# A Hymba layer in fp32 on one core: memory projections first, norms in place with later transposes, GLA decays one pair ahead

## The chip, the core and the metric

The kernel runs on one core of one Trainium2 chip. The metric is the device time of one execution in microseconds (us); given are the median of three executions and one execution under the hardware profiler. The engines are TensorE (PE in the profile, PEld its weight loads), VectorE (DVE), ScalarE (ACT), GpSimd (POOL) and SyncE (SP, which here only issues DMAs).

## The reference

One decoder layer over 512 tokens of width 2048, everything in float32:

```python
xn = rms_norm(h, attn_norm_g)
proj = xn @ w_in
(gq, gk, gv, gg, ga, fq, fk, fv, fg, ff, mq, mg) = jnp.split(proj, _split_points(), axis=-1)
log_a = jax.nn.log_sigmoid((ga @ gla_a_w2 + gla_a_b)) / GLA_TAU
gla_o = gla_chunked(gq, gk, gv, log_a)               # 8 heads, keys of 64, values of 128
fq_h, fk_h = rms_norm(fq, fox_q_norm_g), rms_norm(fk, fox_k_norm_g)
log_f = jax.nn.log_sigmoid(ff + fox_f_b)
fox_o = forgetting_attention(fq_h, fk_h, fv, log_f)   # 4 heads, causal softmax with decays
mn = rms_norm(mem, mem_norm_g)                        # 256 memory tokens
mk, mv = jnp.split(mn @ w_mem_kv, 2, axis=-1)
mk, mq_h = rms_norm(mk, mem_k_norm_g), rms_norm(mq, mem_q_norm_g)
mem_o = softmax(mq_h @ mk.T / sqrt(128)) @ mv         # 4 heads, no mask
o = rms_norm(concat([gla_o, fox_o, mem_o]), out_norm_g)  # per head of 128
gate = concat([silu(gg), sigmoid(fg), sigmoid(mg)])
h = h + (o * gate) @ w_out
u = relu(rms_norm(h, mlp_norm_g) @ w_up)
h = h + (u * u) @ w_down
```

## The kernel before

**Arithmetic.** A float32 product is made of three matmuls of a rounded format (`mm3`, lines 156 to 158): high by high, high by low, low by high. Every weight tile is loaded raw by SP (line 147), rounded by ACT into its high part (148), and DVE takes the remainder as the low part (149). A projection step multiplies one 128-row slice of x by one weight tile: 12 matmuls of 128x512.

**Stages.** First `project` makes gk and gq, and meanwhile `x_sums(0)` and `x_sums(1)` load x again and add its quarters, which the next stage needs. Then four `in_pair` products (gla values, and fq with fk) run by a seven-product scheme whose sums and differences DVE makes. A narrow projection `small` follows. From there to the output projection two generators are interleaved by the code: `projections()` yields after each 12 matmuls, and `steps()` runs the attention work, each `yield n` asking for n such pieces before its next step. After that come the output projection (out0 and on) and the two MLP products.

**What sets the order.** PE runs its matmuls in the order in which the code wrote them, frozen by dependencies. DVE, ACT, POOL and SP run in the order that the tile framework's scheduler gave by priorities: a weight's load and split are put forward (`AHEAD`). An engine does not look past the instruction at its head. In this middle stage there are two buffers of split weights (`n_hl = 2`) and three of raw ones. PSUM is in two pools of four banks: `gbank` for projections, `abank` for attention.

**The projections** are fv, mq, mkv (memory keys and values, 16 tiles of 12 matmuls), then the four gates gg0, gg1, fg and mg. After each gate group `gate` (line 1014) scales it out of PSUM into z, applies log-sigmoid (574, 575), an exponential and for gg a product with z (1018), multiplies the head outputs (1019), and forms the quarter sums s (243) that the output projection needs; some go out to DRAM. Its z uses the buffers of bT and eb.

**The attention steps.** `first_steps` scales gk and gq (651) and makes lf, the log of FoX's forget gates (656). `gla` runs over four chunks of 128 tokens. `decays` makes cumulative logs b; then seven block sizes ("levels") are handled in pairs: `level` takes differences (719, 720), an exponential on ACT (721) and products with q and k (ql 725, e 731); `level_scores` makes scores on PE (lp, 737) and `place_scores` copies them under a mask (746). Then o, the state st and, for chunks before the last, the next decays. `norms` and `turned_heads` normalize heads: four squares with sums on ACT, a reciprocal root on DVE and ACT (118 to 124), a product (590), and after some yields the transposes on PE (tps 603, ot 944) and a scaled copy by ACT (946). `Fox` and `Mem` are softmax attention in banks of logits: lg on PE, ls on DVE (841), p on ACT (890), its transposes pT (898), the product av (909). Memory's keys are normalized by `memory_norms`, which starts from squares of memory (199, 200) that each memory tile adds beside its projection. `place` fetches head sums back for the output projection.

Of the kernel before, what the change touches and what calls it, by code (L numbers as in the profile page):

```python
# [12 lines left out]
ALU = mybir.AluOpType  # L13
# [33 lines left out]
def hybrid_layer(  # L47
# [289 lines left out]
    def multiply(w, after, inside=None):  # L337
# [230 lines left out]

    def log_sigmoid(dst, z, e):
# [5 lines left out]
        V.scalar_tensor_tensor(dst, z, 0.0, e, op0=ALU.min, op1=ALU.subtract)  # L575
# [16 lines left out]
    def norms(srcs, gain, dsts, name, wait):  # L592

        for a in range(0, len(srcs), 2):
            r = head_rms(srcs[a : a + 2], f"{name}{a}")
            nrm = [tmp(f"nrm_{name}{a + i}", "tc") for i in range(2)]
            for i in range(2):
                normed(nrm[i], srcs[a + i], r[:, 4 * i : 4 * i + 4])
            yield wait
            for i in range(2):  # L600
                tps = abank(f"tps_{name}{a + i}")
                for h in range(4):
                    T.transpose(tps[:, h * 128 : h * 128 + 128], nrm[i][:, h * 128 : h * 128 + 128], ident)
                A.activation(dsts[a + i], tps.rearrange("p (h t) -> p h t", h=4), AF.Copy, scale=gain)
# [35 lines left out]
    def first_steps():  # L640
        G.memset(gaT, 1.0)
        V.tensor_mul(gaT[:16, :], nps[32:48, :], rbx[32:48, :])
        lfT = tmp("lfT", "td")[:FH, :]
# [8 lines left out]
        yield 2  # L652
# [6 lines left out]
        g = decay_logs(0)  # L659
        yield from norms([o[:, t, 1024:1536] for t in range(NT)], gains[:, 0:1], tokens(fqT), "fq", 2)  # L660
# [9 lines left out]
        return g  # L670
# [40 lines left out]
    def level(c, li, bT):  # L711
# [5 lines left out]
        e = tmp(f"e_{c}_{B}", "ta")  # L717
# [3 lines left out]
        A.activation(e, e, AF.Exp)  # L721
        ql = qls[li % 2]
# [7 lines left out]

        V.tensor_mul(ev[:, :, :hb], ev[:, :, :hb], blocks_of(kTs[:, c, :], B)[:, :, :hb])
# [21 lines left out]
    def gla(g):  # L753
        state = tmp("state", "rbx")
        bT, eb, kd = decays(0, g)
        for c in range(NT):
# [3 lines left out]
            ready = [level(c, li, bT) for li in (0, 1)]  # L760
            yield 2 if c else 3
            for a in (0, 2, 4, 6):
# [3 lines left out]
                if a == 6:  # L766
# [15 lines left out]
                yield 3 if a in (0, 4) else 2  # L782
# [33 lines left out]
            if c == 0:  # L816
                yield from norms([o[:, t, 1536:2048] for t in range(NT)], g_fk, tokens(fkT), "fk", 1)
# [36 lines left out]
    class Mem:  # L854
# [12 lines left out]
        def v(self, s, h):  # L867
            return late["mv"][:, s, h * 128 : h * 128 + 128]
# [64 lines left out]
    def turned_heads(n, wait):  # L933

        ot = o[:, :, n * 512 : n * 512 + 512]
        for a in (0, 2):
            r = head_rms([ot[:, a + i, :] for i in range(2)], f"on_{n}_{a}")
            for i in range(2):
                normed(ot[:, a + i, :], ot[:, a + i, :], r[:, 4 * i : 4 * i + 4])
        yield wait  # L940
# [8 lines left out]
    mem_ready = []  # L949
    late = {}  # L950

    def memory_norms():
        mkv = bigt(1, [128, 2, 1024], "mkv")
        mkT = late["mkT"] = mkv[:, 0, :].rearrange("p (h m) -> p h m", h=MH)
        mv = late["mv"] = mkv[:, 1, :].rearrange("p (m c) -> p m c", m=MT)
        mqT = late["mqT"] = bigt(0, [128, 4, S], "mqT")
        mrstd = token_rstd(macc, MT, "mem")
        mks = room.rearrange("p (m c) -> p m c", m=MT)
        for m in range(MT):
            V.tensor_scalar(mks[:, m, :], mks[:, m, :], mrstd[:, m : m + 1], None, op0=ALU.mult)  # L960
            A.activation(mv[:, m, :], mraw[:, m, :], AF.Copy, scale=mrstd[:, m : m + 1])
        dsts = [mkT[:, :, m * 128 : m * 128 + 128] for m in range(MT)]
        yield from norms([mks[:, m, :] for m in range(MT)], g_mk, dsts, "mk", 2)
        yield 1
        yield from norms([o[:, t, 1536:2048] for t in range(NT)], gains[:, 1:2], tokens(mqT), "mq", 2)

    def steps():
        g = yield from first_steps()
        yield 2
        yield from gla(g)  # L970
        assert mem_ready
        yield 1
# [464 lines left out]
```

## Time and profile before

| quantity | value |
|---|---|
| median of 3 executions | 2209.38 us (2209.36 to 2211.11) |
| profiled execution | 2212.2 us |
| its span in the trace | 2210.5 us |
| PE, DVE, ACT, POOL busy | 2130.1, 1617.7, 1142.7, 195.5 us |
| mean clock granted to PE | 0.983 of full |

The span is from the first to the last instruction of the profiled execution. "Busy" leaves out waiting. A releaser, written with an arrow (`<-`), is the instruction on another engine that ended a wait.

### The profile page before, as it was taken

What the parts mean: (1) busy time and instruction counts of PE and PEld (TensorE: products, weight loads), DVE (VectorE), ACT (ScalarE), POOL (GpSimd) and SP (SyncE); (2) the same over time, 40 slices, a digit from 0 to 9 for tenths busy, and PEclk for the clock granted to TensorE, in tenths of its full rate; (3) what the DMA queues carried; (4) which work ended last, traced back from release to release, by engine and by line L of the source; (5) the groups of instructions that cost most, each with busy time, mean ns of one, the idle gap of its engine ahead of it and who ended that gap; (6) DMA issues with size and microseconds to landing.
All of it is one profiled execution on the core that took longest, in us unless ns stands there. A gap on an engine that the chain in (4) does not pass through costs nothing.

```text
span 2210.5 us, 25633 instructions
## 1 busy us (share of the span) xinstructions
PE 2130.1 (96%) x9746; PEld 1747.9 (79%) x9746; DVE 1617.7 (73%) x1711; ACT 1142.7 (52%) x1715; POOL 195.5 (9%) x239
## 2 busy tenths in 40 slices
PE   8999999897979989999999999999999999999999
PEld 7887688786767778878888888888788788788787
DVE  7689766865364498887677767769868768777875
ACT  6553442535365465655555555556645546546543
POOL 0433100000000003100000000000010000000000
PEclk9999999998989999999999999999999999999999
DMA  7443222421232566624534533445586677678654
GB/s 268 143 157 101 95 65 70 142 78 60 67 100 77 180 223 225 238 87 142 190 125 142 190 127 141 171 161 190 201 228 187 199 204 229 165 198 243 187 170 131
DMA packets 77988, 348.15 MB, mean 157 GB/s; under 512 B 9241, under 2 KB 11289, under 8 KB 56362
## 3 DMA queue, kind: packets, MB, share of 16 engines
q1 hardware_dynamic: 57770, 275.22, 36.0%
q0 software_dynamic: 20096, 71.31, 12.3%
q8 instruction: 76, 1.25, 0.2%
q14 instruction: 46, 0.38, 0.1%
HBM read 271.00 MB, written 75.50 MB: 157 GB/s over the span
## 4 chain that ended last, share of the span: by engine, by line
PE 79%; DVE 10%; DMA 4%; ACT 3%; issue 3%; SPq 0%; DVEq 0%; ACTq 0%
PE acc_up L156 9%; PE acc_up L158 9%; PE acc_up L157 9%; PE acc_dn L157 7%; PE acc_dn L158 7%; PE acc_dn L156 7%; PE acc_out L157 2%; PE acc_out L156 2%; PE acc_out L158 2%; DMA left1l<-op 2%; DVE hl_hl_in L333 2%; DVE hl_dn L333 1%; PE gg L156 1%; DVE raw_dn L295 1%; PE gg L158 1%
## 5 line engine op out<-in xcount | busy, mean ns | idle before, releaser
L333 DVE TENSOR_TENSOR hl_up<-raw_up,hl_up 128x1024 fp32r<-128x1024 f32 x224 | 271.8, 1223 | 144.0 <-ACT hl_up L333 143.8
L333 ACT CAST hl_up<-raw_up 128x1024 fp32r<-128x1024 f32 x224 | 235.3, 1052 | 256.2 <-PE acc_up L158 196.3
L333 DVE TENSOR_TENSOR hl_dn<-raw_dn,hl_dn 128x1024 fp32r<-128x1024 f32 x224 | 270.6, 1222 | 99.2 <-ACT hl_dn L333 98.4
L333 ACT CAST hl_dn<-raw_dn 128x1024 fp32r<-128x1024 f32 x224 | 234.6, 1054 | 209.3 <-PE acc_dn L158 160.2
L295 DVE TENSOR_TENSOR raw_dn<-raw_dn,raw_dn 128x2048 f32<-128x2048 f32 x64 | 146.1, 2287 | 15.9 <-DMA raw_dn<-in_w_down_dram 15.6
L295 DVE TENSOR_TENSOR raw_up<-raw_up,raw_up 128x2048 f32<-128x2048 f32 x64 | 145.2, 2269 | 0.2 <-DMA raw_up<-in_w_up_dram 0.2
L333 ACT CAST hl_out<-raw_out 128x1024 fp32r<-128x1024 f32 x56 | 58.6, 1052 | 56.9 <-PE acc_out L158 36.4
L1352 POOL DMA_DIRECT2D hd<-m x48 | 41.5, 865 | 518.4 <-ACT m L1351 518.4
L333 DVE TENSOR_TENSOR hl_out<-raw_out,hl_out 128x1024 fp32r<-128x1024 f32 x56 | 70.3, 1272 | 15.3 <-ACT hl_out L333 15.2
L1351 ACT COPY m<-acc_dn 128x512 f32<-128x512 f32 x96 | 54.5, 587 | 30.4 <-PE acc_dn L158 30.4
L1244 POOL DMA_DIRECT2D op<-u x32 | 17.1, 533 | 491.8 <-ACT u L1253 482.5
L156 PE MATMUL gg<-ahi_x,hl_gg 128*128 128x512 f32 x128 | 53.6, 418 | 6.6 <-DVE z_gg L1014 6.6
L157 PE MATMUL acc_dn<-hl_dn,left 128*128 128x512 f32 x128 | 50.3, 393 | 4.5 <-DVE hl_dn L333 4.5
L157 PE MATMUL acc_dn<-hl_dn,left0h 128*128 128x512 f32 x128 | 50.5, 395 | 3.2 <-DVE hl_dn L333 3.2
L156 PE MATMUL acc_up<-hl_up,left 128*128 128x512 f32 x128 | 50.6, 395 | 3.1 <-ACT z L1307 3.1
L157 PE MATMUL acc_in<-hl_hl_in,sh 128*128 128x512 f32 x128 | 50.4, 394 | 2.9 <-DVE hl_hl_in L333 2.9
L333 ACT CAST hl_hl_in<-spare 128x1024 fp32r<-128x1024 f32 x31 | 32.5, 1050 | 36.0 <-PE acc_in L158 14.9
L158 PE MATMUL gg<-ahi_x,hl_gg 128*128 128x512 f32 x128 | 51.0, 398 | 0.0
L157 PE MATMUL gg<-alo_x,hl_gg 128*128 128x512 f32 x128 | 50.9, 398 | 0.0
L157 PE MATMUL acc_dn<-hl_dn,left3h 128*128 128x512 f32 x128 | 50.8, 397 | 0.0
L156 PE MATMUL acc_dn<-hl_dn,left3h 128*128 128x512 f32 x128 | 50.7, 396 | 0.0
L156 PE MATMUL acc_up<-hl_up,left0h 128*128 128x512 f32 x128 | 50.5, 394 | 0.0
(565 smaller groups left out, 6329.5 us busy)
## 6 DMA issues: line engine op xcount, KB each, us to landing
raw_up<-in_w_up_dram SPq DMA_DIRECT2D x64, 1024.0 KB, 4.9
raw_dn<-in_w_down_dram SPq DMA_DIRECT2D x64, 1024.0 KB, 7.0
hd<-m POOLq DMA_DIRECT2D x48, 512.0 KB, 5.4
raw_out<-in_w_out_dram SPq DMA_DIRECT2D x16, 1024.0 KB, 4.8
op<-u POOLq DMA_DIRECT2D x32, 512.0 KB, 3.5
op<-s POOLq DMA_DIRECT2D x24, 512.0 KB, 3.3
spare<-in_w_pair_dram SPq DMA_DIRECT2D x16, 512.0 KB, 4.1
raw_in<-in_w_pair_dram SPq DMA_DIRECT2D x16, 512.0 KB, 4.2
```

What stands on the lines that cost most here:

```text
L156: T.matmul(ps, lhsT=ah, rhs=bh, start=start, stop=False, skip_group_check=on)
L157: T.matmul(ps, lhsT=ah, rhs=bl, start=False, stop=False, skip_group_check=on)
L158: T.matmul(ps, lhsT=al, rhs=bh, start=False, stop=stop, skip_group_check=on)
L295: V.tensor_sub(dst, a, b)
L333: made = A.copy(hi, part), V.tensor_sub(lo, part, hi.bitcast(F32))
L1244: nc.gpsimd.dma_start(down_op[c][i][:, half * 1024 : half * 1024 + 1024], tile)
L1351: A.copy(st[:, t * 512 : t * 512 + 512], acc[t])
L1352: nc.gpsimd.dma_start(dst, st.rearrange("p (t n) -> p t n", t=2), accum_op=ALU.add)
```

## The change

1. **Memory square sums.** All of memory is loaded and squared between the two halves of the x sums, and its reciprocal root `mrstd` is made there. Memory is loaded a second time for its projection, which no longer adds squares; its results leave PSUM through ACT, scaled by `mrstd`. `memory_norms` is gone.
2. **Order of projections.** mkv goes first, then fv, mq, gg0, gg1, fg, mg.
3. **Norms** overwrite their source. `turn` transposes it several steps later, out of `beside` in GLA, or one tile at each step of the FoX loop. For some heads ACT makes one square of 512 columns and DVE reduces it.
4. **GLA levels.** Differences and exponential (`level`) are made one pair ahead; the products with q and k (`level_rows`) follow after the scores of the pair before. All waits are `yield 2`.
5. **mg** projects into `abank`. In the output projection, products 1 and 5 exchange pools.
6. **Early fetches** of `place` are issued by POOL instead of SP. Some temporaries change tags.

```diff
@@ before the pairs
     with tc.high_priority(offset=400):
         x_sums(0)
+    macc = spare[:, 3072 : 3072 + M]
+    for k in range(NK):
+        mt = tmp(f"memT_{k}", "ta", M)
+        nc.sync.dma_start(mt, memT[k])
+        add_squares(macc, mt, k == 0, f"mem{k}")
+    mrstd = token_rstd(macc, MT, "mem")
     x_sums(1)
@@ multiply
-                chain[p] = [(gbank if p == (5 if w.name == "out0" else 1) else abank)(...) for i in range(2)]
+                chain[p] = [(gbank if p == 1 else abank)(...) for i in range(2)]
@@ norms
+    def norms(*srcs, on_act=True):
+        r = head_rms(srcs, f"n{next(count)}", on_act)
+        for i, src in enumerate(srcs):
+            normed(src, src, r[:, 4 * i : 4 * i + 4])
+    def turn(src, gain, dst):
+        i = next(count)
+        tps = abank(f"tps_{i}")
+        for h in range(4):
+            T.transpose(tps[:, h * 128 : h * 128 + 128], src[:, h * 128 : h * 128 + 128], ident)
+        A.activation(dst, tps.rearrange("p (h t) -> p h t", h=4), AF.Copy, scale=gain)
@@ first_steps
-        yield 2
+        yield 3
+        g = decay_logs(0)
+        for t in (0, 2):
+            norms(o[:, t, 1024:1536], o[:, t + 1, 1024:1536])
+        yield 3
@@ gla
-            ready = [level(c, li, bT) for li in (0, 1)]
-            yield 2 if c else 3
+            ready = [level_rows(c, *level(c, li, bT)) for li in (0, 1)]
+            ahead = [level(c, li, bT) for li in (2, 3)]
+            yield 2
             for a in (0, 2, 4, 6):
                 lps = [(li, level_scores(c, li, e, ql)) for li, e, ql in ready]
...
+                ready = [level_rows(c, *v) for v in ahead]
                 for li, lp in lps:
                     place_scores(li, lp)
-                ready = [level(c, li, bT) for li in (a + 2, a + 3) if li < len(LEVELS)]
+                ahead = [level(c, li, bT) for li in (a + 4, a + 5) if li < len(LEVELS)]
...
-                yield 3 if a in (0, 4) else 2
+                beside(c, a)
+                yield 2
+    def beside(c, a):
+        if c == 0 and a in (2, 4):
+            for t in (a - 2, a - 1):
+                turn(o[:, t, 1024:1536], gains[:, 0:1], tokens(fqT)[t])
...
+        if c == 2 and a in (0, 2):
+            head_norms(a // 2, 0, True)
+        if (c, a) == (2, 4):
+            norms(*(mks[:, m, :] for m in range(MT)))
@@ steps
         yield from gla(g)
-        assert mem_ready
-        yield 1
+        head_norms(0, 2)
...
+        head_norms(1, 2)
+        for t in (0, 2):
+            norms(o[:, t, 1536:2048], o[:, t + 1, 1536:2048], on_act=False)
+        yield 2
+        spread(dgs, late["rbg"], "g")
+        yield 2
+        turned_heads(0)
+        yield 1
+        turned_heads(1)
+        beside = [lambda m=m: turn(mks[:, m, :], g_mk, mkT[:, :, m * 128 : m * 128 + 128]) for m in range(MT)]
+        beside += [lambda t=t: turn(o[:, t, 1536:2048], gains[:, 1:2], tokens(mqT)[t]) for t in range(NT)]
+        yield 1
+        for v in softmax_heads([Fox(t) for t in reversed(range(NT))]):
+            if beside:
+                beside.pop(0)()
+            yield v
+        head_norms(2, 0)
+        head_norms(2, 2)
         yield from softmax_heads([Mem(t) for t in range(NT)])
         place()
-        yield from turned_heads(3, 2)
+        head_norms(3, 0)
+        head_norms(3, 2)
+        turned_heads(2)
+        yield 5
+        turned_heads(3)
@@ place
-            fetch(i, cs, out_op[i][:, cs])
+            fetch(i, cs, out_op[i][:, cs], nc.gpsimd)
@@ projections
         for m in range(MT):
-            V.tensor_copy(room[:, m * 512 : m * 512 + 512], mps[m][0])
-            A.copy(mraw[:, m, :], mps[m][1])
+            A.activation(mks[:, m, :], mps[m][0], AF.Copy, scale=mrstd[:, m : m + 1])
+            A.activation(mv[:, m, :], mps[m][1], AF.Copy, scale=mrstd[:, m : m + 1])
...
-        ps = yield from project_steps(gates[3][0], turned=True, order=(0, 7, 6, 5, 4, 3, 2, 1))
+        ps = yield from project_steps(gates[3][0], turned=True, bank=abank, order=(0, 7, 6, 5, 4, 3, 2, 1))
```

Three places show what this does to the engines' queues. The first is DVE in the stage of gk and gq, at the end of `x_sums(0)` (st and sl are its sums, hl_gk and hl_gq weight remainders). Before, the next x sums follow at once:

```order
L403 TENSOR_TENSOR sl_756<-st_0_816,sh 128x2x256
L403 TENSOR_TENSOR sl_757<-st_1_817,sh 128x2x256
L149 TENSOR_TENSOR hl_gq_623<-raw_gq_622,hl_gq_623 128x1024
L243 TENSOR_TENSOR st_0_832<-xs_0_826,xs_1_827 128x256
L243 TENSOR_TENSOR st_1_833<-xs_0_826 128x256
```

Now the adds of memory's squares stand there:

```order
L404 TENSOR_TENSOR sl_756<-st_0_816,sh 128x2x256
L404 TENSOR_TENSOR sl_757<-st_1_817,sh 128x2x256
L201 TENSOR_TENSOR spare<-spare,sq_mem_831 128x256
L150 TENSOR_TENSOR hl_gq_623<-raw_gq_622,hl_gq_623 128x1024
L201 TENSOR_TENSOR spare<-spare,sq_mem_836 128x256
L201 TENSOR_TENSOR spare<-spare,sq_mem_841 128x256
```

Fifteen such adds come in, and the x sums of the second half (the next rows named st) stand behind the last of them.

The second place is PE at the end of the first gate projection, gg0 (bank 3 gets its last three matmuls) and the start of gg1. Before, the transposes of head group 0 (ot) stand between:

```order
L156 MATMUL gg_3_3561<-ahi_x_679,hl_gg_3942 128x512
L157 MATMUL gg_3_3561<-alo_x_680,hl_gg_3942 128x512
L158 MATMUL gg_3_3561<-ahi_x_679,hl_gg_3942 128x512
L944 MATMUL ot_0_4034<-ident,o 128x128 x4
L944 MATMUL ot_1_4035<-ident,o 128x128 x4
L944 MATMUL ot_2_4036<-ident,o 128x128 x4
L944 MATMUL ot_3_4037<-ident,o 128x128 x4
L156 MATMUL gg_0_4161<-ahi_x_125,hl_gg_4166 128x512
```

Now it is a step of the FoX loop: the product of one bank, the transposes of the next, the logits (lg) of the tenth.

```order
L157 MATMUL gg_3_3836<-ahi_x_679,hl_gg_4409 128x512
L158 MATMUL gg_3_3836<-alo_x_680,hl_gg_4409 128x512
L159 MATMUL gg_3_3836<-ahi_x_679,hl_gg_4409 128x512
L957 MATMUL av_f_3_4518<-o,pTs_f_3_4436 128x128 x3
L946 MATMUL pT_f_0_4525<-ident,p_f_0_4448 128x128 x4
L878 MATMUL lg_f_2_4532<-fkT,fqT 128x256
L881 MATMUL lg_f_2_4532<-rows_r,negid 128x256
L157 MATMUL gg_0_4543<-ahi_x_125,hl_gg_4548 128x512
```

The transposes of head groups 0 and 1 have moved into gg0, some ten steps earlier, and the gate of gg0 now has FoX steps on both sides.

The third place is DVE at the end of the gate of gg0: products of the gate (ee, o), sums for the output projection (s), and ls, the masked logits. Before, the masked logits were those of FoX's first bank:

```order
L1018 TENSOR_TENSOR ee_gg_3_4137<-ee_gg_3_4137,z_gg_3_4136 128x512
L1019 TENSOR_TENSOR o<-o,ee_gg_3_4137 128x512
L243 TENSOR_TENSOR s_gg_4146<-o 128x512
L243 TENSOR_TENSOR s_gg_4149<-o 128x512
L243 TENSOR_TENSOR s_gg_4147<-s_gg_4146,o 128x512
L841 ISA ls_0_4211,nmx_f_0_4207<-lg_f_0_4208,cmask 128x512
```

Now they are those of the tenth bank:

```order
L1064 TENSOR_TENSOR o<-o,ee_gg_2_4484 128x512
L585 SCALAR_TENSOR_TENSOR ee_gg_3_4494<-z_gg_3_4493,ee_gg_3_4494 128x512
L1063 TENSOR_TENSOR ee_gg_3_4494<-ee_gg_3_4494,z_gg_3_4493 128x512
L1064 TENSOR_TENSOR o<-o,ee_gg_3_4494 128x512
L244 TENSOR_TENSOR s_gg_4503<-o 128x512
L244 TENSOR_TENSOR s_gg_4506<-o 128x512
L244 TENSOR_TENSOR s_gg_4504<-s_gg_4503,o 128x512
L895 TENSOR_TENSOR ls_2_4537<-lg_f_2_4532,cmask 128x512
```

In both kernels an ls stands behind the gate's products; what has moved is which bank it belongs to, and what PE has to do until it needs that bank.

More of the change, by code (lines that the diff above doesn't have):

```diff
@@ L1 @@
+import itertools
 from contextlib import ExitStack
@@ L348, in multiply @@
             if q == 0 and first:
-                chain[p] = [(gbank if p == (5 if w.name == "out0" else 1) else abank)(f"acc_{w.name}_{p}_{i}") for i in range(2)]
+                chain[p] = [(gbank if p == 1 else abank)(f"acc_{w.name}_{p}_{i}") for i in range(2)]
             acc = chain[p if first else 5 if p == 3 else 1]
@@ L590, in normed @@
         V.tensor_mul(heads4(dst), heads4(src), r.unsqueeze(2).broadcast_to([128, 4, 128]))
[L592 to L604, printed above, removed]
+    def norms(*srcs, on_act=True):
[5 more added lines that the diff above has]
+        tps = abank(f"tps_{i}")
+        for h in range(4):
+            T.transpose(tps[:, h * 128 : h * 128 + 128], src[:, h * 128 : h * 128 + 128], ident)
+        A.activation(dst, tps.rearrange("p (h t) -> p h t", h=4), AF.Copy, scale=gain)
     def tokens(w):
@@ L658, in first_steps, with forget @@
         V.tensor_copy(lf, lps[:, : NT * FH])
-        g = decay_logs(0)
-        yield from norms([o[:, t, 1024:1536] for t in range(NT)], gains[:, 0:1], tokens(fqT), "fq", 2)
+        late["lf"] = lf
+        return g
+    def forget():
+        lf = late["lf"]
         cps = abank("cT")
@@ L931, in hybrid_layer, with turned_heads @@
     heads_of = {}
-    def turned_heads(n, wait):
+    def turned_heads(n):
         ot = o[:, :, n * 512 : n * 512 + 512]
[L936 to L940, printed above, removed]
         banks = [abank(f"ot_{n}_{i}") for i in range(4)]
@@ L967, in steps @@
     def steps():
         g = yield from first_steps()
-        yield 2
         yield from gla(g)
-        assert mem_ready
-        yield 1
+        head_norms(0, 2)
         late["rbg"] = tmp("rbg", "rbx")
         tp.tile([128, 40], F32, tag="fill", name="fill_tp", bufs=1)
-        spread(spread_dg(xrstd, "g"), late["rbg"], "g")
-        for n in range(2):
-            yield from turned_heads(n, 2)
-        yield from softmax_heads([Fox(t) for t in reversed(range(NT))])
-        yield from memory_norms()
@@ L981, in steps @@
+        beside += [lambda t=t: turn(o[:, t, 1536:2048], gains[:, 1:2], tokens(mqT)[t]) for t in range(NT)]
[6 more added lines that the diff above has]
+        head_norms(2, 2)
         yield from softmax_heads([Mem(t) for t in range(NT)])
         place()
-        yield from turned_heads(3, 2)
-    def project_steps(group, turned=False, order=range(NK // 2)):
+        head_norms(3, 0)
@@ L987, in project_steps @@
+        head_norms(3, 2)
+        turned_heads(2)
+        yield 5
+        turned_heads(3)
+    def project_steps(group, turned=False, bank=gbank, order=range(NK // 2)):
         first_k, last_k = 2 * order[0], 2 * order[-1] + 1
-        ps = [gbank(f"{group}_{t}") for t in range(NT)]
+        ps = [bank(f"{group}_{t}") for t in range(NT)]
         for kp in order:
```

89 lines of the change are left out of this document (45 added, 44 removed).

## The prediction

> **What bounds the kernel now.** I read the page first, for the engine that is busy longest.
>
> ```profile
> PE 2130.1 (96%) x9746; PEld 1747.9 (79%) x9746; DVE 1617.7 (73%) x1711; ACT 1142.7 (52%) x1715; POOL 195.5 (9%) x239
> ```
>
> TensorE (PE) is busy for 2130.1 of 2210.5 us. The diff moves PE's matmuls and takes none away, so all that can be won is the 80 us in which PE idles, and whatever PE runs slowly. The table of PE's waits says where it idles (what waits, for what, us in total, times, longest).
>
> ```profile
> PE ot L944 <- DVE o L590: 10.4, 3, 4.6
> PE gg L156 <- DVE z_gg L1014: 6.6, 1, 6.6
> PE lp L737 <- DVE e L731: 5.6, 2, 4.6
> PE tps_mk L603 <- DVE nrm_mk L590: 5.0, 1, 5.0
> PE tps_mq L603 <- DVE nrm_mq L590: 5.0, 1, 5.0
> PE mg L156 <- DVE z_fg L1014: 4.5, 2, 3.6
> PE lf L656 <- DVE lfT L575: 3.6, 1, 3.6
> PE acc_out L156 <- DVE x L1168: 3.1, 1, 3.1
> PE acc_out L157 <- DVE hl_out L333: 3.0, 2, 1.8
> PE acc_in L157 <- DVE hl_hl_in L333: 2.9, 4, 1.5
> PE acc_out L156 <- ACT left3h L1029: 2.0, 1, 2.0
> PE pT_f L898 <- ACT p_f L890: 1.9, 1, 1.9
> ```
>
> Four kinds of place show: transposes that wait for a normalization (ot, tps_mk, tps_mq), level scores that wait for their decays (lp), projections that wait for a PSUM bank which a gate still holds (gg, mg), and the start of the output projection (three acc_out rows). The first three kinds lie in the stretch that the change rewrites. Next I read PE's own rows around the largest, since the table gives only the idle part (start, duration, what, in brackets the idle time before).
>
> ```profile
> 522.05 0.39 PE L157 MATMUL gg<-alo_x,hl_gg 128*128 128x512 f32 x1
> 522.28 0.39 PE L158 MATMUL gg<-ahi_x,hl_gg 128*128 128x512 f32 x1
> 526.69 0.98 PE L944 MATMUL ot<-ident,o 128*128 128x128 f32 x2 [4.02 <-DVE o L590]
> ...
> 542.20 0.80 PE L156 MATMUL gg<-ahi_x,hl_gg 128*128 128x512 f32 x1 [6.56 <-DVE z_gg L1014]
> 542.79 0.63 PE L157 MATMUL gg<-alo_x,hl_gg 128*128 128x512 f32 x1
> 543.22 0.63 PE L158 MATMUL gg<-ahi_x,hl_gg 128*128 128x512 f32 x1
> ```
>
> A warm projection matmul starts 0.23 us after the one before it (522.05 to 522.28); after the long wait the step is 0.43 us (542.79 to 543.22). So a wait of several microseconds is paid twice: the idle time, then five to thirteen matmuls, or a set of transposes, at half pace. Read this way, the eight long waits up to the output projection (lf, the second lp, ot of head groups 0 and 3, gg, tps_mk, tps_mq, mg) have an afterpay of 2.3 to 4.4 us each, about 26 us. The idle part is the first seven rows and pT_f, 42.6 us, and some 2.4 us of waits under a microsecond. **Together these places hold about 71 us.** The windows of 25 us say the same (PE, PE load, DVE, ACT, POOL busy with counts, clock granted, DMA share, GB/s).
>
> ```profile
> 88.00:110.00 22.00, 22.00 (x102) 18.33 (x101) 15.99 (x24) 11.94 (x18) 14.91 (x30) 1.00 0.13 44
> 130.00:145.00 15.00, 15.00 (x68) 12.43 (x67) 14.86 (x10) 8.27 (x11) 6.49 (x2) 1.00 0.00 1
> 525.00:550.00 25.00, 14.34 (x50) 10.36 (x51) 17.45 (x43) 20.38 (x68) 1.07 (x2) 0.66 0.10 31
> 775.00:800.00 25.00, 18.11 (x65) 13.80 (x64) 24.87 (x28) 11.69 (x16) 3.26 (x6) 0.86 0.48 165
> ```
>
> In 525 to 550 neither VectorE (DVE, 17.45) nor ScalarE (ACT, 20.38) is full: PE waits there for a serial chain, not for a full engine. That is what moving work apart can mend. In 775 to 800 DVE is full, and the change takes nothing from it.
>
> **Why the clock matters to the sum.** Waits of 1.9 us and less (pT_f) leave the step at 0.23 us; waits of 3.6 us and more do not. The Trainium skill ("TensorE: Matmul & The Clock Gate", Part 1: The HAM clock gate) says that PE's clock halves after an idle window of about 3.4 us, free-running, and comes back after about as long busy; the trace agrees as far as those rows go. By that rule two waits of 2.8 and 1.1 us apart, as I expect at the first gate below, are not followed by slow matmuls; if they were, the sum would be some 2.6 us higher.
>
> **The change, part by part.**
>
> 1. *Norms ahead of their transposes.* The three ot waits, tps_mk and tps_mq go: 20.4 us idle and their slow matmuls, 9.8 + 7.7 + 8.1 + 7.3 = 32.9 us. What hides the norms now: for heads 0 and 1 there are 48 projection matmuls and a spread between the last GLA output and the first transpose, 48 x 0.227 + 0.8 = 11.7 us, and by my count of the chain (squares, a reciprocal root, two products) the norm is done about 9 us after that output. For head group 3, 36 matmuls (8.2 us) lie between. If a cover fell short, one of the old waits, 7 to 10 us, would be back.
>
> 2. *lf.* It now stands behind 72 projection matmuls instead of 24, and the norm squares no longer stand before it on ACT: its 3.6 us and what followed go, 7.0 us in all.
>
> 3. *Decays one pair ahead.* The waits of lp (1.05 and 4.56 us, 1.2 + 9.0 with what followed) came where memory tiles lay beside GLA. The same load now comes earlier, in chunk 0, so it must be costed for a pair of levels. DVE's groups there (count | busy, mean ns | its idle before):
>
> ```profile
> L746 DVE COPY_PREDICATED scores<-lmask,lp 128x512 f32<-128x512 int32 x28 | 24.8, 885 | 20.3 <-PE lp L737 20.2
> L725 DVE TENSOR_TENSOR ql<-qTs,e 64x256 f32<-64x256 f32 x56 | 24.4, 435 | 5.4 <-ACT e L721 4.5
> L149 DVE TENSOR_TENSOR hl_mem<-raw_mem,hl_mem 128x1024 fp32r<-128x1024 f32 x16 | 19.5, 1221 | 2.4 <-ACT hl_mem L148 2.3
> L731 DVE TENSOR_TENSOR e<-e,kTs 128x256 f32<-128x256 f32 x28 | 12.5, 460 | 1.0 <-ACT e L721 0.7
> L719 DVE TENSOR_TENSOR e<-bT 128x256 f32<-128x256 f32 x28 | 11.9, 424 | 0.2
> L167 DVE SCALAR_TENSOR_TENSOR meml<-spare,colt,memh 128x256 fp32r<-128x256 f32 x14 | 6.7, 481 | 7.3 <-ACT memh L166 7.2
> ```
>
> Two levels cost 2 x (2 x 0.424 + 2 x 0.435 + 0.460 + 0.885) = 6.13 us (the differences come in two halves, of which the row shows one), two memory tiles 2 x (1.221 + 0.481) = 3.40. Rows of DVE overlap by about 0.08 us each (in the rows of part 5 a product of 0.68 us at 550.64 is followed at 551.25, 0.61 on), and there are 16 of them: about 8.2 us of DVE for two levels with two tiles. PE's side is 24 matmuls and two score sets.
>
> ```profile
> 318.97 1.95 PE L737 MATMUL lp<-ql,e 128*128 128x128 f32 x16
> 320.67 0.48 PE L156 MATMUL fv<-hl_fv,ahi_x 128*128 128x512 f32 x1
> ```
>
> The score sets take 320.67 - 318.97 = 1.70 us, so PE needs 5.44 + 1.70 = 7.14 us. DVE is behind by about a microsecond a pair for four pairs, and gains on the steps without levels (72 matmuls before lf, then the output and state of chunk 0); over the whole stage I count 45 us of DVE against 48.5 of PE. The square sums' adds, of the shape of those differences and so 0.42 us a tile, are no longer in that load. So something between 1 (DVE never last) and 12 us (one wait like that of 4.56 with its slow matmuls, and two of a microsecond): I take **+4**, nearer the low end since DVE has the smaller total. Under fv and mq the weights cost 1.22 per 24 matmuls, DVE 6.1 of 7.14 us: no waits for lp there.
>
> 4. *Memory square sums in the pair stage.* They add 16 loads of 128 KB, 16 squares on ACT and 15 adds on DVE, 15 x 0.42 = 6.3 us, and push the second half of the x sums, their loads on SP and their sums, behind them. DVE has 6 us free in 88 to 110 but none in 130 to 145 (14.86 of 15). Ends: -1 (one of the four acc_in waits goes) and +8 (all 6.3 us arrive on a full DVE, and the longest acc_in wait, 1.5 us, doubles). I take **+2**.
>
> ```profile
> L333 DVE TENSOR_TENSOR hl_hl_in<-spare,hl_hl_in 128x1024 fp32r<-128x1024 f32 x10 | 12.2, 1224 | 5.3 <-ACT hl_hl_in L333 5.3
> L333 DVE TENSOR_TENSOR hl_hl_in<-raw_in,hl_hl_in 128x1024 fp32r<-128x1024 f32 x5 | 8.9, 1777 | 4.7 <-ACT hl_hl_in L333 4.7
> ```
>
> The same operation took 1.22 us in ten instances and 1.78 on average in five others of that stage, where POOL is at work too. The Trainium skill ("Advanced Engine Details and Errata", VectorE Performance Modes) says that the second Vector port is shared with GpSimd and that the two block each other; by that rule POOL work pushed later would lengthen five more products, 5 x 0.55 = 2.8 us, and the sum would be 2171. The trace shows the longer products, not their cause.
>
> 5. *Gates.* mg now has banks of its own pool (abank), so its 4.5 us and the slow matmuls go, 7.75 us. Gate 0 now falls inside the FoX loop, and its own wait remains. DVE today:
>
> ```profile
> 536.45 1.29 DVE L590 TENSOR_TENSOR o<-o,hr_on 128x512 f32<-128x512 f32 x2
> 537.66 1.29 DVE L575 SCALAR_TENSOR_TENSOR ee_gg<-z_gg,ee_gg 128x512 f32<-128x512 f32 x2
> ...
> 549.43 1.29 DVE L243 TENSOR_TENSOR s_gg<-o 128x512 f32<-128x512 f32 x2
> 550.64 0.68 DVE L243 TENSOR_TENSOR s_gg<-s_gg,o 128x512 f32<-128x512 f32 x1
> 551.25 0.68 DVE L841 CUSTOM_DVE_ANT_0 ls<-lg_f,cmask 128x512 f32<-128x512 f32 x1
> ```
>
> Two normalizations stood ahead of the gate; they are gone from there, but the later z still need a buffer that the gate frees: I count 2.8 + 1.1 us of idle. Then a **new wait**: in the new order the masked logits of the tenth FoX bank (ls) stand on DVE behind the whole gate: 19 wide products at 0.60 and one weight remainder, 13.5 us, with about 4 us of round trips to ACT. PE reaches that bank's pT_f after 12 matmuls and the two short waits, about 8.7 us on; pT_f is 8.8 us late, and 2.3 us go to slow matmuls. Gate 0 costs **15**, against 9.7 for gg and 2.0 for pT_f and its neighbour today. Gate 1 now stands right before fg, where transposes used to cover it. Its wait is taken as that of gg without the normalizations: 6.56 - 1.29 = 5.2 us, and 2.1 slow, **+7.3** (bounds 0 and 10).
>
> 6. *The rest.* The three early fetches on POOL have over 100 us until the output projection, nothing. Scaling mks and mv straight from PSUM takes four copies from DVE and adds none to PE. Other small waits at new seams: **+1.5**. The start of the output projection, 3.1 + 3.0 + 2.0 us idle, 11 with slow matmuls, stays.
>
> **The sum.** -71 of old places, and + 4 + 2 + 15 + 7.3 + 1.5 = +29.8: **-41 us**, of the profiled span of 2210.5 us. That execution took 2212.2 us, 2.8 over the median of 2209.4; on the median 2209.4 - 41 = 2168.
>
> **Rivals.**
> - *The tenth bank isn't held by gate 0* (10%): the scheduler's order is on paper, and pT_f could be covered as it nearly is today. Then 15 becomes 5.5: 2158 us.
> - *The new seams are at their upper ends* (15%): memory tiles +12, squares +8, gate 1 at 10. 2168 + 8 + 6 + 3 = 2185 us. For it: DVE at 14.86 of 15, and 8.2 against 7.14 us a pair. Against: both stages have slack ahead.
> - *Slower: memory tiles can't be made in time* (4%). With two weight buffers a tile's cast (1.05) and remainder (1.22) follow one another after the tile two before is used; a tile is only 12 matmuls, 2.72 us. If DVE's queue delays every remainder, each of the eight pairs idles like lp did at its worst, 9.0 us with its slow matmuls: 72 - 4 = 68 more, 2236 us. It decides from 5.7 us a pair (45 / 8), that is when DVE's 8.2 us a pair becomes about 13.
> - *The waits only change names* (4%): the norms, earlier, are late all the same as ACT is at 20.38 of 25 around the gates; then 33 us stay and the time is 2201 to 2209.
>
> **How the numbers follow.** The forecast as worked out has 67%. Measurement can tell about 0.2%, 4.4 us, from no change. Faster by more than that: 0.67 + 0.10 + 0.15 and the faster part of the last rival, 0.94; within: 0.02; slower: 0.04. The range takes both first rivals and the bounds of terms 3 to 5: 2146 to 2194 us.
>
> **What would show it.** Right: in the new table of PE's waits no ot, no tps, no lf and no mg row above 1 us; a pT_f row of about 9 us in the FoX loop just after gate 0; fg waiting about 5 us for z_gg; lp waits only in the first 50 us after the pair stage; the three acc_out rows unchanged; a granted clock of 1.00 where the first heads are turned, which had 0.66. Wrong: acc_in rows above 10 us in total (term 4), mkv waiting for hl_mem again and again (the slower rival), ot or tps rows still there (the covers of part 1), no pT_f row (the new wait).

## The result and the profile after

| | before | after |
|---|---|---|
| median | 2209.55 us (4 runs, 2209.36 to 2211.11) | 2171.84 us (4 runs, 2169.68 to 2176.02) |
| ratio to before | | 0.983, 95% interval 0.9813 to 0.9847 |
| span of the profiled run | 2210.5 us | 2168.0 us |
| clock granted | 0.983 | 0.989 |

The kernel is 37.7 us faster, 3.3 us short of the forecast gain of 41. The page's first part and the table of PE's waits of the changed kernel (what waits, for what, us in total, times, longest):

```profile
PE 2114.0 (98%) x9746; PEld 1739.7 (80%) x9746; DVE 1616.8 (75%) x1723; ACT 1135.0 (52%) x1603; POOL 192.0 (9%) x236
...
PE pT_f L946 <- ACT p_f L938: 8.2, 1, 8.2
PE fg L157 <- DVE z_gg L1059: 6.2, 1, 6.2
...
PE acc_in L158 <- DVE hl_hl_in L334: 5.0, 5, 1.4
...
PE acc_out L157 <- DVE x L1211: 3.3, 1, 3.3
...
PE gg L157 <- DVE z_gg L1059: 3.1, 2, 2.8
...
PE acc_out L158 <- DVE hl_out L334: 2.2, 2, 1.8
PE acc_out L157 <- ACT left3h L1074: 2.0, 1, 2.0
PE acc_in L157 <- ACT o L451: 0.9, 1, 0.9
PE lp L764 <- DVE e L758: 0.9, 1, 0.9
```

The rows of ot, tps, lf and mg are gone. New are pT_f with 8.2 us and fg with 6.2. The three acc_out rows still stand (3.3, 2.2 and 2.0 us, 8.1 before and 7.5 now), and acc_in has grown from 2.9 to 5.0. In the windows of 25 us the idle stretch around the gates has become shorter and has moved:

```profile
525.00:550.00 25.00, 21.93 (x97) 16.12 (x97) 14.00 (x28) 14.62 (x28) 0.77 (x1) 0.91 0.17 52
550.00:575.00 25.00, 16.81 (x67) 13.33 (x67) 10.43 (x19) 5.70 (x17) 3.64 (x6) 0.61 0.24 83
625.00:650.00 25.00, 18.76 (x84) 14.98 (x83) 20.65 (x34) 18.33 (x32) 2.48 (x4) 0.86 0.26 79
```

The last row is the wait of fg. In 550 to 575 (PE 16.81, DVE 10.43, ACT 5.70) all engines have time left, and the clock is at 0.61: PE waits for one late instruction. It is the masked logits of FoX's tenth bank, in DVE's rows at 556.67 (start, duration, what):

```profile
555.47 0.68 DVE L244 TENSOR_TENSOR s_gg<-o 128x512 f32<-128x512 f32 x1
556.07 0.68 DVE L244 TENSOR_TENSOR s_gg<-s_gg,o 128x512 f32<-128x512 f32 x1
556.67 0.68 DVE L895 TENSOR_TENSOR ls<-lg_f,cmask 128x512 f32<-128x512 f32 x1
557.27 0.68 DVE L244 TENSOR_TENSOR s_gg<-o,s_gg 128x512 f32<-128x512 f32 x1
```

ACT makes p from them at 558.58, and PE takes up its transposes at 559.24, after 8.19 us of idle:

```profile
559.24 1.18 PE L946 MATMUL pT_f<-ident,p_f 128*128 128x128 f32 x4 [8.19 <-ACT p_f L938]
```

To compare stages I took when a tile's first matmul starts in each trace. Differences between two such starts, in us:

| stretch on PE | before | before, 2nd profile | after | predicted change | measured, first two profiles |
|---|---|---|---|---|---|
| pair stage (acc_in to small) | 156.7 | 157.6 | 161.3 | +2 | +4.6 |
| memory and GLA (spread_x to gg) | 197.5 | 196.7 | 194.0 | | -3.5 |
| gg to mg | 242.5 | 242.6 | 220.4 | -27.8 with the row above | -22.1 |
| mg to acc_out | 60.8 | 60.8 | 43.6 | -15.4 | -17.2 |
| acc_out to acc_up | 171.0 | 171.0 | 171.4 | 0 | +0.4 |
| acc_up to the end | 1274.8 | 1271.1 | 1269.8 | 0 | -5.0 |

The second and third row are to be read together, since the rest of GLA's last chunk, which ran beside gg, now comes ahead of it. The transposes of head group 3, 1.8 us of PE work, moved from the stretch of mg into that of gg to mg; set right for that, the two are -27.4 and -15.4 against -27.8 and -15.4. The last row can't be put down to the change: see ctrl_before.

### The profile page after: what moved, and what is told of

It is laid out like the page before. It is cut to its first block, busy times and chain, and to the rows that moved or that the text cites. A ratio compares the mean times of both kernels' runs of the same rounds, so it can differ in the third digit from the quotient of the medians.

```text
span 2168.0 us, 25541 instructions
## 1 busy us (share of the span) xinstructions
PE 2114.0 (98%) x9746; PEld 1739.7 (80%) x9746; DVE 1616.8 (75%) x1723; ACT 1135.0 (52%) x1603; POOL 192.0 (9%) x236
## 4 chain that ended last, share of the span: by engine, by line
PE 79%; DVE 10%; DMA 5%; issue 3%; ACT 2%; POOL 1%; SPq 0%; ACTq 0%; DVEq 0%; POOLq 0%
PE acc_up L157 9%; PE acc_up L158 9%; PE acc_up L159 9%; PE acc_dn L158 7%; PE acc_dn L159 7%; PE acc_dn L157 7%; PE acc_out L158 2%; PE acc_out L157 2%; PE acc_out L159 2%; DMA left1l<-op 2%; DVE hl_hl_in L334 1%; DVE hl_dn L334 1%; PE gg L157 1%; DVE raw_dn L296 1%; PE gg L159 1%
## 5 line engine op out<-in xcount | busy, mean ns | idle before, releaser
L158 PE MATMUL acc_in<-hl_hl_in,sh 128*128 128x512 f32 x128 | 50.5, 395 | 5.0 <-DVE hl_hl_in L334 5.0
L334 DVE TENSOR_TENSOR hl_hl_in<-spare,hl_hl_in 128x1024 fp32r<-128x1024 f32 x31 | 44.1, 1433 | 11.0 <-ACT hl_hl_in L334 11.0
L157 PE MATMUL acc_in<-hl_hl_in,sh 128*128 128x512 f32 x128 | 49.9, 390 | 0.9 <-ACT o L451 0.9
```

What stands on the lines that cost most here:

```text
L157: T.matmul(ps, lhsT=ah, rhs=bh, start=start, stop=False, skip_group_check=on)
L158: T.matmul(ps, lhsT=ah, rhs=bl, start=False, stop=False, skip_group_check=on)
L334: made = A.copy(hi, part), V.tensor_sub(lo, part, hi.bitcast(F32))
```

## Experiments

Each kernel is an edit of the changed kernel, unless something else is said. In the first group the changed kernel itself took 2172.2 us, before 2210.49 us.

**ctrl_after**, no edit.

> The changed kernel once more, as the reference point of this group of runs. Both theories: 2168 to 2176 us, 0.982 to 0.985 of before; the PE waits pT_f 8.2, fg 6.2, gg 3.1 us again.

Measured: 2172.2 us, ratio 0.9825 (0.9812 to 0.9838), pT_f 8.2, fg 6.2, gg 3.1.

**sums_td**, the place of the tenth bank's logits.

```diff
-            return halves(tmp(f"{v}_{group}", "td" if v in ("s2", "s4") else "tb" if last else "ta"))
+            return halves(tmp(f"{v}_{group}", "td" if v in ("s2", "s4") or n == 0 else "tb" if last else "ta"))
```

> The quarter sums s1 and s3 of gate 0 take buffers of the tag td instead of ta, which FoX's masked logits use too; with that the tenth bank's logits stand on DVE right behind the second z of gate 0 instead of behind the whole gate. Theory (the wait of pT_f is the tenth bank's place in DVE's queue, and that place comes from the shared buffers): the 8.2 us of pT_f fall below 1 us, with about 3 to 4 us of slow matmuls behind it; 10 to 12 us faster than the changed kernel, some 2160 us. Rival (the gate's chain is late in any case, and whoever comes next waits): pT_f falls, but gg or the next bank waits as much longer; within 3 us of the changed kernel.

Measured: 2160.2 us, ratio 0.9771 (0.9758 to 0.9785), 12 us below ctrl_after. pT_f is down to 0.4 us; fg (6.1) and gg (4.0) stay. The theory holds: DVE makes the tenth bank's logits 4.8 us after it starts the first z of gate 0 (537.46 us), instead of 20.1 us after it:

```profile
542.30 0.69 DVE L895 TENSOR_TENSOR ls<-lg_f,cmask 128x512 f32<-128x512 f32 x1 [0.18 <-PE lg_f L881]
```

The run shows that the shared buffers held ls back. The reason is read from the code, not measured: buffers of one tag are given out in program order, the sums s1 and s3 come before the tenth ls there, and so ls could not be placed ahead of their first instructions, however early its logits were ready.

**z_four**, the bank that fg waits for.

```diff
-            z = tmp(f"z_{group}_{i}", "ta" if last else ("bT", "eb")[i % 2])
+            z = tmp(f"z_{group}_{i}", "ta" if last or n == 1 and i > 1 else ("bT", "eb")[i % 2])
```

> The third and fourth z of gate 1 take buffers of the tag ta, so that all four banks of gg1 are scaled out of PSUM at once. Theory (fg waits because the third z waits for the first one's buffer): fg's 6.2 us go, and 1.5 us of slow matmuls, 7 to 8 us faster than the changed kernel. Rival (the wait is the gate's work on ACT and DVE, and fg or a transpose waits for its end): a wait of 4 us or more appears at fg's or ot's rows; within 3 us of the changed kernel.

Measured: 2161.78 us, ratio 0.9776 (0.9763 to 0.9789), 10 us below ctrl_after, a little more than expected; fg's row is gone and no row took its place. From gg to mg it took 211.5 us against 220.4: 8.9 us for this wait and what followed.

**gates_free**, both, and the same for gate 0's z.

```diff
-            z = tmp(f"z_{group}_{i}", "ta" if last else ("bT", "eb")[i % 2])
+            z = tmp(f"z_{group}_{i}", "ta" if last or n < 2 and i > 1 else ("bT", "eb")[i % 2])
...
-            return halves(tmp(f"{v}_{group}", "td" if v in ("s2", "s4") else "tb" if last else "ta"))
+            return halves(tmp(f"{v}_{group}", "td" if v in ("s2", "s4") or n == 0 else "tb" if last else "ta"))
```

> Both edits together, and the third and fourth z of gate 0 in ta too. Theory: the waits pT_f, fg and gg all go, 17.5 us idle and 5 to 7 us of slow matmuls: 22 to 25 us faster than the changed kernel, some 2148 us, and no granted clock below 0.95 between 540 and 650 us. Rival (the waits move on): 10 to 15 us faster at most, with a new wait above 3 us in the FoX loop.

Measured: 2148.49 us, ratio 0.972 (0.9707 to 0.9734), 23.7 us below ctrl_after; from gg to mg 197.4 us. Its windows where the changed kernel idled:

```profile
525.00:550.00 25.00, 25.00 (x123) 18.69 (x122) 14.91 (x32) 14.40 (x31) 0.77 (x1) 1.00 0.13 43
550.00:575.00 25.00, 22.52 (x115) 18.26 (x114) 19.90 (x42) 14.48 (x38) 3.67 (x6) 1.00 0.35 118
625.00:650.00 25.00, 25.00 (x117) 20.81 (x116) 13.36 (x18) 11.02 (x17) 2.59 (x4) 1.00 0.43 140
```

The clock stays at 1.00, and PE has small waits only (the largest there are 1.1 us of pT_f and 1.3 of pT_m). So the cost of both gates was in the buffers: the same work is done, and PE no longer waits for it.

The second group undoes one part of the change each (before in these runs: 2208.73 us).

**mg_gbank**, mg's banks.

```diff
-        ps = yield from project_steps(gates[3][0], turned=True, bank=abank, order=(0, 7, 6, 5, 4, 3, 2, 1))
+        ps = yield from project_steps(gates[3][0], turned=True, order=(0, 7, 6, 5, 4, 3, 2, 1))
...
-                chain[p] = [(gbank if p == 1 else abank)(...) for i in range(2)]
+                chain[p] = [(gbank if p == (5 if w.name == "out0" else 1) else abank)(...) for i in range(2)]
```

> The changed kernel with mg in gbank again, and products 1 and 5 of the output projection in their former pools. Theory (mg's bank was what it waited for): mg waits for z_fg again, 4 to 6 us idle and about 3 us of slow matmuls, 6 to 9 us slower than the changed kernel (2172), some 2180 us. Rival (with the transposes of head group 3 in fg, gate 2 is early enough that the pool doesn't matter): within 3 us.

Measured: 2176.5 us, ratio 0.9845 (0.9831 to 0.9858). The wait is back, smaller than before the change, and mg to acc_out takes 49.7 us instead of 43.6:

```profile
688.45 0.80 PE L157 MATMUL mg<-ahi_x,hl_mg 128*128 128x512 f32 x1 [2.76 <-DVE z_fg L1059]
689.05 0.63 PE L158 MATMUL mg<-alo_x,hl_mg 128*128 128x512 f32 x1
```

By the stretch the theory holds with its low end, 6.1 us. The median is only 4.7 us above the changed kernel's 2171.84, and the intervals of the two ratios overlap, so the whole times alone don't decide.

**squares_back**, the square sums beside memory's projection; keys and values leave PSUM unscaled and are scaled in place in chunk 1.

```diff
     with tc.high_priority(offset=400):
         x_sums(0)
...
-    for k in range(NK):
-        mt = tmp(f"memT_{k}", "ta", M)
-        nc.sync.dma_start(mt, memT[k])
-        add_squares(macc, mt, k == 0, f"mem{k}")
-    mrstd = token_rstd(macc, MT, "mem")
     x_sums(1)
...
                 split_gain(mt, g_mem[:, k : k + 1], mh, ml)
+                add_squares(macc, mt, k == 0, f"mem{k}", room[:, 3 * M :])
...
     def beside(c, a):
+        if (c, a) == (1, 0):
+            mrstd = token_rstd(macc, MT, "mem")
+            for m in range(MT):
+                V.tensor_scalar(mks[:, m, :], mks[:, m, :], mrstd[:, m : m + 1], None, op0=ALU.mult)
+                A.activation(mv[:, m, :], mv[:, m, :], AF.Copy, scale=mrstd[:, m : m + 1])
...
-            A.activation(mks[:, m, :], mps[m][0], AF.Copy, scale=mrstd[:, m : m + 1])
-            A.activation(mv[:, m, :], mps[m][1], AF.Copy, scale=mrstd[:, m : m + 1])
+            A.activation(mks[:, m, :], mps[m][0], AF.Copy)
+            A.activation(mv[:, m, :], mps[m][1], AF.Copy)
```

> The changed kernel with memory's squares added beside its projection again, as before the change; the reciprocal root is made early in GLA's chunk 1 and scales keys and values in place there. Theory (the squares cost the pair stage about 5 us, and DVE has 48.5 - 45 us to spare beside memory): small starts 4 to 5 us earlier than 257.6 us, lp and mkv wait 0 to 3 us more; 1 to 5 us faster than the changed kernel. Rival (6.7 us more of DVE overload the memory stage): lp or mkv rows of 5 us or more, 3 to 12 us slower. If the pair stage's waits come from elsewhere, small starts at 257 us all the same.

Measured: 2172.37 us, ratio 0.9831 (0.9817 to 0.9844): no change, from two halves of which each theory had one. small begins at 253.8 us instead of 257.6:

```profile
L157 PE MATMUL small<-ahi_x,hl_small x16: 387/396/402, 253.8 to 264.2; 128*48 128x512 f32 x16
```

but spread_x to gg takes 201.7 us instead of 194.0, with waits of b, tps and lp in it, the first of them:

```profile
286.75 1.67 PE L700 MATMUL b<-tri,g 128*128 128x128 f32 x8 [2.37 <-DVE g L580]
```

So the squares cost 4 us where they are, and about 7.7 beside memory's projection. The scaling in place is hardly in that: the last of these waits ends at 317.6 us, and ACT scales the values at 358 us. The wait of lp is as long as in the changed kernel (1.0 and 0.9 us); the new ones are b, 2.4 us, and tps, 1.3.

**levels_late**, no lead of one pair.

```diff
-            ahead = [level(c, li, bT) for li in (2, 3)]
...
-                ready = [level_rows(c, *v) for v in ahead]
                 for li, lp in lps:
                     place_scores(li, lp)
-                ahead = [level(c, li, bT) for li in (a + 4, a + 5) if li < len(LEVELS)]
+                ready = [level_rows(c, *level(c, li, bT)) for li in (a + 2, a + 3) if li < len(LEVELS)]
```

> The changed kernel with each pair of levels made whole after the scores of the pair before, as before the change. Theory (the lead of one pair is what removed the lp waits): lp waits return beside the memory tiles of chunk 0, where DVE has 8.2 us of work for PE's 7.1 a pair: 4 to 12 us slower than the changed kernel. Rival (moving memory and the squares was enough): lp below 2 us in total, within 3 us.

Measured: 2172.86 us, ratio 0.9831 (0.9818 to 0.9845). The rival holds, but for 0.3 us of lp: spread_x to gg takes 195.8 us, 1.8 more, where the theory said 4 to 12, and lp waits 2.3 us in two places:

```profile
297.63 1.13 PE L764 MATMUL lp<-ql,e 128*128 128x128 f32 x8 [0.95 <-DVE e L758]
306.48 1.13 PE L764 MATMUL lp<-ql,e 128*128 128x128 f32 x8 [1.33 <-DVE e L758]
```

**mkv_last**, the former order of projections.

```diff
     def projections():
-        mps = [[gbank(f"mkv_{m}_{n}") for n in range(2)] for m in range(MT)]
...
         ps = yield from project_steps("fv")
...
         ps = yield from project_steps("mq")
...
+        mps = [[gbank(f"mkv_{m}_{n}") for n in range(2)] for m in range(MT)]
...
-        if (c, a) == (2, 4):
-            norms(*(mks[:, m, :] for m in range(MT)))
...
         head_norms(1, 2)
+        norms(*(mks[:, m, :] for m in range(MT)))
```

> The changed kernel with the projections in their former order fv, mq, mkv; memory's key norms then come after GLA. Theory (the order matters little once levels are one pair ahead and no squares are added): lp and mkv below 3 us in total, -3 to +4 us to the changed kernel. Rival (memory first is what removed the lp waits): lp waits of 4 us or more under mkv in chunks 2 and 3, 5 to 12 us slower.

Measured: 2172.77 us, ratio 0.9833 (0.9819 to 0.9846). spread_x to gg takes 197.2 us, 3.2 more, with one lp wait of 2.7 us, and the norm of memory's keys, now after GLA, makes ot wait 1.8 us:

```profile
439.21 1.07 PE L764 MATMUL lp<-ql,e 128*128 128x128 f32 x6 [2.70 <-DVE e L758]
...
487.68 0.63 PE L985 MATMUL ot<-ident,o 128*128 128x128 f32 x4 [1.81 <-DVE z_n L123]
```

That is within the bounds of the theory (lp below 3 us in total). The order is worth a few microseconds in these stretches, too few to tell in the whole time.

The third group (before: 2209.82 us):

**short_cover**, less work between the norms and their transposes.

```diff
-        yield 2
+        yield 1
         spread(dgs, late["rbg"], "g")
-        yield 2
         turned_heads(0)
-        yield 1
+        yield 4
         turned_heads(1)
```

> The changed kernel with the transposes of head group 0 after only 12 gate matmuls and the spread, 3.5 us behind GLA's last output instead of 11.7; group 1 at its place. Theory (the norm's chain takes about 9 us, and the matmuls put between hide it): ot waits about 5 us for the norm, with about 3 us of slow matmuls: 6 to 10 us slower than the changed kernel, some 2180 us. Rival (the norms are quick when they are issued ahead of everything else): ot below 2 us, within 3 us.

Measured: 2180.66 us, ratio 0.987 (0.9855 to 0.9885), 9 us above the changed kernel:

```profile
479.56 0.33 PE L987 MATMUL ot<-ident,o 128*128 128x128 f32 x1 [4.54 <-DVE o L604]
480.16 2.18 PE L987 MATMUL ot<-ident,o 128*128 128x128 f32 x9 [0.27 <-DVE o L604]
```

The norm is as long as in the changed kernel: from GLA's last output on PE to the end of the second product of head group 0 it takes 8.9 us in both traces (469.3 to 478.2 there, 471.2 to 480.1 here). The 11.7 us of matmuls hide it.

**fetch_sp**, the early fetches on SP: `fetch(i, cs, out_op[i][:, cs])` without the queue.

> The changed kernel with the three early fetches issued by SP again. Theory (they have over 40 us until the output projection needs them): within 3 us of the changed kernel, the acc_out waits unchanged. Rival (SP's queue of weight loads is held by them): mg or acc_out wait 3 us or more for weights.

Measured: 2168.74 us, ratio 0.982 (0.9804 to 0.9837), the acc_out waits as they were. No difference that can be told.

**ctrl_before**, the kernel before once more.

> The kernel before once more, for a second profile of it: from the first matmul of the up projection to the end it took 1274.8 us in its profile, the changed kernel 1269.8, though neither the diff nor the prediction touches that part. Theory (that part varies from run to run): 1268 to 1273 us. Rival (the change makes it faster): 1274 us or more again.

Measured: 1271.1 us from acc_up to the end. In the twelve profiles of these runs the stretch took 1267.1 to 1272.6 us, whatever the edit; the first profile of before, 1274.8, is the highest of all. So nothing shows that the 5.0 us between the two first profiles are the change's; the second profile of before is 1.3 us from the changed kernel's.

**best**, gates_free with the squares in another place.

```diff
-    for k in range(NK):
-        mt = tmp(f"memT_{k}", "ta", M)
...
-    mrstd = token_rstd(macc, MT, "mem")
     x_sums(1)
...
     def beside(c, a):
+        if c == 1:
+            for k in range(2 * a, 2 * a + 4):
+                mt = spare[:, 3072 + M : 3072 + 2 * M]
+                nc.sync.dma_start(mt, memT[k])
+                add_squares(macc, mt, k == 0, f"mem{k}", mt)
+        if (c, a) == (2, 2):
+            mrstd = token_rstd(macc, MT, "mem")
+            for m in range(MT):
+                V.tensor_scalar(mks[:, m, :], mks[:, m, :], mrstd[:, m : m + 1], None, op0=ALU.mult)
+                A.activation(mv[:, m, :], mv[:, m, :], AF.Copy, scale=mrstd[:, m : m + 1])
...
-            A.activation(mks[:, m, :], mps[m][0], AF.Copy, scale=mrstd[:, m : m + 1])
-            A.activation(mv[:, m, :], mps[m][1], AF.Copy, scale=mrstd[:, m : m + 1])
+            A.activation(mks[:, m, :], mps[m][0], AF.Copy)
+            A.activation(mv[:, m, :], mps[m][1], AF.Copy)
```

> gates_free with memory's squares written into GLA's chunk 1 instead of ahead of the second half of the x sums; the scheduler then puts the adds one by one between the x sums, which keep their place. Keys and values are scaled in place in chunk 2. Theory (the pair stage lost its 4.5 us because the x sums stood behind the squares): from the first pair product to small 157 to 158 us instead of 161 to 162, and 3 to 5 us faster than gates_free, some 2144 us. Rival (the adds themselves are too much for DVE there, wherever they stand): 161 us or more, no faster than gates_free (2148).

Measured: 2144.21 us, ratio 0.9708 (0.9694 to 0.9722): the fastest median of all. From the first pair product, at 97.5 us, to small it took 157.3 us, as before the change, with all fifteen adds made before GLA starts:

```profile
L157 PE MATMUL small<-ahi_x,hl_small x16: 387/396/402, 254.8 to 265.3; 128*48 128x512 f32 x16
```

The x sums of the second half are back in their place. One of the four sums that DVE makes of each slice of x (times in us: first and last start), before, in the changed kernel and here:

```profile
L243 DVE TENSOR_TENSOR st<-xs x8: 417/420/2626, 46.6 to 85.8; 128x256 f32<-128x256 f32 x8
L244 DVE TENSOR_TENSOR st<-xs x8: 411/418/2616, 45.4 to 109.2; 128x256 f32<-128x256 f32 x8
L244 DVE TENSOR_TENSOR st<-xs x8: 415/417/2618, 46.4 to 86.4; 128x256 f32<-128x256 f32 x8
```

In the changed kernel the last of them starts at 109.2 us, and three waits of acc_in before 150 us (0.9, 0.6 and 1.3 us) are there which neither before nor best has. So the adds were not too much for DVE; the x sums that stood behind them were late. The stretch shows it (157.3 against 162.3 in gates_free); the whole times, 2144.21 and 2148.49, have intervals that overlap.

## Why the prediction was right, point by point

- **Norms ahead of their transposes, -32.9.** Right: no ot, tps row is left, and short_cover brings 4.5 us of ot back when the cover shrinks to 3.5 us, as the chain of about 9 us said (8.9 measured).
- **lf, -7.0.** Right, the row is gone. Which of its two reasons did it, the later place or the norm squares behind it, was not tried apart.
- **Levels, -10.2 and +4.** The waits of lp went, and the +4 was too much: what is left of lp is one wait of 0.9 us, 40 us behind the start of small. Which of three edits removed those waits is open. Undone alone, the lead of one pair costs 1.8 us in the stretch (lp 2.3), the order of projections 3.2 (lp 2.7), the square adds 7.7, but at b and tps, not at lp. No one of them brings back the 5.6 us of lp, and all three undone together was not tried. What is shown is that the square adds, whose leaving this load the prediction noted in a side remark, are the dearest of the three when they stand there.
- **Squares in the pair stage, +2, bounds -1 and +8.** Too small: 4.6 us, and squares_back gives back 4 of them. The step that was mis-sized counted DVE's free time; what counted was who stands behind: the prediction named the x sums behind the adds, but gave their lateness no price. best has the same adds between the x sums and loses nothing. The 2.8 us more by five longer products did not come: from 88 to 262 us nine of DVE's remainders for the pair products took over 1.5 us before, and eight after the change.
- **Gate 0, 15, and gate 1, 7.3.** Right in place and size. pT_f waited 8.2 us (8.8 forecast), fg 6.2 (5.2), the z of gate 0 2.8 and 0.3 (2.8 and 1.1). Together they cost 23.0 us by gates_free (22.3 forecast), gate 1 alone 8.9 by z_four (7.3), the tenth bank alone 11.4 by sums_td. One sum in the working is off: 19 products at 0.60 and a remainder of 1.22 make 12.6 us, not 13.5, and with that the wait of pT_f would have been put at 7.9 us, nearer still.
- **mg, -7.75.** Right for this change; the stretch of mg lost what the two waits in it had cost. But with the other parts of the change in place its pool is worth 6.1 us only, since its wait shrinks from 4.5 to 3.1.
- **Fetches on POOL, nothing; output projection unchanged.** Right.
- **Clock.** Right where the first heads are turned: 1.00 from 475 to 500 us. Wrong in one place: the wait of 2.8 us was followed by slow matmuls (below). Six of them took 0.2 us more each, and the product behind them, av_f, 1.91 us, where the next ones take 1.05. The total can have lost about 0.9 us by it: PE then waited for DVE anyway, and DVE had lost 0.86 us to that late product.

```profile
551.09 0.42 DVE L965 TENSOR_TENSOR o<-av_f,rc_f 128x256 f32<-128x256 f32 x1 [0.86 <-PE av_f L957]
```

None of the rivals came true. The tenth bank was held by gate 0. Memory tiles and gate 1 stayed below their upper ends, and the squares reached a little over half of their +8. No mkv row came, and no ot or tps row was left.

From spread_x to acc_out the forecast was -43.2 us and the profiles have -42.8. That it is so near is in part luck, since errors cancel. The slow matmuls of the old places, put at 26 us, were about 22: PE was busy for 44.4 us at a granted clock of 0.50 there, and half of that is an estimate of the loss. Against that, memory tiles and new seams, put at +4 and +1.5, left only 1.05 us of idle.

The forecast of 2168 is 3.8 us below the median. The pair stage makes 2.6 of it. The profiled run, 2169.68, is the fastest of the four, so part of the rest is spread between runs.

## What to carry to other kernels

A wait for a serial chain goes by work put between, and how much is needed is read from the chain, 9 us here, not from engines' busy shares. Before code is put ahead of something, ask what then stands behind it on every queue: fifteen adds cost 4 us ahead of the x sums and nothing that can be seen between them. Where a late instruction was ready long before, look at the buffers that it shares with the work ahead of it: two tags were worth 23 us, more than half of what the whole change brought.

## What was not expected of the hardware

Slow matmuls followed shorter waits than I had seen before. In the changed kernel, after 2.79 us of idle:

```profile
545.77 0.79 PE L157 MATMUL gg<-ahi_x,hl_gg 128*128 128x512 f32 x1 [2.79 <-DVE z_gg L1059]
546.36 0.63 PE L158 MATMUL gg<-alo_x,hl_gg 128*128 128x512 f32 x1
546.78 0.63 PE L159 MATMUL gg<-ahi_x,hl_gg 128*128 128x512 f32 x1
```

The step is 0.42 us. In sums_td the same place waited 2.99 us and went on at 0.23, and became slow only behind a second wait of 0.96:

```profile
546.85 0.50 PE L157 MATMUL gg<-ahi_x,hl_gg 128*128 128x512 f32 x1 [2.99 <-DVE z_gg L1059]
547.19 0.39 PE L158 MATMUL gg<-alo_x,hl_gg 128*128 128x512 f32 x1
547.42 0.40 PE L159 MATMUL gg<-ahi_x,hl_gg 128*128 128x512 f32 x1
548.78 0.75 PE L157 MATMUL gg<-ahi_x,hl_gg 128*128 128x512 f32 x1 [0.96 <-DVE z_gg L1059]
549.33 0.63 PE L158 MATMUL gg<-alo_x,hl_gg 128*128 128x512 f32 x1
```

The clock of these traces changes in steps of 3.41 us. In the changed kernel it falls at 545.36 us, in sums_td at 548.85. The windows of one step before and after, the first two rows from the changed kernel, the other three from sums_td (length, PE's busy time, and as before; the clock is the third figure from the right):

```profile
541.94:545.36 3.42, 1.04 (x5) 0.51 (x3) 2.59 (x5) 2.48 (x5) 0.00 (x0) 1.00 0.50 153
545.36:548.77 3.41, 2.72 (x6) 1.72 (x7) 2.94 (x5) 2.93 (x5) 0.77 (x1) 0.50 0.04 13
542.02:545.43 3.41, 1.84 (x7) 1.10 (x7) 3.13 (x6) 3.30 (x8) 0.00 (x0) 1.00 0.51 154
545.43:548.85 3.42, 1.04 (x4) 0.56 (x4) 3.29 (x7) 2.90 (x7) 0.43 (x1) 1.00 0.00 0
548.85:552.26 3.41, 3.41 (x13) 3.12 (x14) 1.52 (x3) 2.31 (x5) 0.34 (x1) 0.50 0.25 82
```

In both kernels the clock fell behind a step in which PE had been busy for 1.04 us. In sums_td the wait of 2.99 us lay across two steps, so PE was busy for 1.84 us in the first and kept its clock; the wait of 0.96 us then fell into the second. In the fourteen profiles of this case the clock fell 103 times, 102 of them behind a step with at most 1.57 us of PE work, and it never held behind one with less than 1.52 (the ends of matmuls are modelled, so these two figures are estimates).

The Trainium skill ("TensorE: Matmul & The Clock Gate", Part 1: The HAM clock gate) asks for an idle window of about 3.4 us, free-running. That the same wait may or may not slow what follows fits a free-running window; that 2.8 us suffice does not fit a window that must be idle throughout. By these rows a wait from somewhat under 3 us on can bring slow matmuls, and where it lies in the steps decides.
